# A decoder layer's opening: c sent to all partitions by DMA, a full-width first rstd row, TensorE on zeros, and two chunks instead of three

## The chip, the cores and the metric

One core of one Trainium2 chip. The metric is the device time of one execution in microseconds. TensorE is called PE (PEld for its weight loads), VectorE DVE, ScalarE ACT, GpSimd POOL, and SyncE, which issues every DMA of this kernel, SP.

## The reference

A decoder layer for 256 tokens of width 2048 in float32: a SwiGLU, a token mixer, a second SwiGLU, each behind an RMSNorm whose shift, scale and gate come from a conditioning vector c. Only the first SwiGLU's opening is touched:

```python
cond = jax.nn.silu(c)
mod = cond @ ada_w[l] + ada_b[l]            # 9 x 2048 numbers
sh1, sc1, gt1, ... = jnp.split(mod, N_MOD, axis=-1)
y = x * rsqrt(mean(x * x) + EPS) * norm_g   # per token
h = y * (1 + sc1) + sh1
x = x + 0.5 * gt1 * ((silu(h @ wg) * (h @ wu)) @ wd)
```

Here h is 256 x 2048, wg and wu are 2048 x 5632, wd is 5632 x 2048.

## The kernel before, in words

Activations stand feature-major: x is 16 slices (k = 0 to 15) of 128 features by 256 tokens. A float32 product is made of two parts each: hs holds each slice of h as a high and a low half, and each weight tile (128x128) is split into whi and wlo.

*Weights.* They come in blocks of 8 tiles, 512 KB, in the order of use (`Stream.next`): SP issues the DMA into `wraw`, ACT casts it to `whi` (L94), DVE subtracts to get `wlo` (L97). Each of the three rotates over three tiles, and every fourth block has a tile of its own, so a block reuses the place of the one four before it.

*adaLN columns.* A column is 128 numbers of mod. `ada_col` sends 1 MB of ada_w (128 features x 2048) by DMA and multiplies and sums it against silu(c), held in `cs` on all partitions, in one DVE pass (L204). The first four have tiles of their own (`adaf`); the others rotate over two (`adat`). The order is scale and shift of slice 0, of slice 1, and so on: 32 columns for SwiGLU_1's h, then the gates. Columns are recorded beside the weights at a rate per block (`RATE`, 0.45 at first), or at once where a slice is about to be used (`ada_need`). When a slice's second column is done, `modulate_one` makes it: the gain g (L302), ht = x times gain times the rstd row (L289), hs on ACT and its low half on DVE.

*First row.* Until then: c goes to one partition, POOL broadcasts it, ACT applies Silu. ACT squares x, DVE sums the squares to two slices, `norm_rstd` contracts them against two columns of ones into rstd as a column per token, and turns it into a row on all partitions by two more matmuls (L275, L276, copied in L281).

*The first half of SwiGLU_1* (`gate_up_first`, 28 feature groups f of 128, g and u each) contracts in chunks of slices, so that PE can begin before all of h is there: for each chunk all 28 f, in groups of 8 with a PSUM bank (`pgu`) each. In the first group of a chunk the first LEAD slices are taken slice by slice over all 8 f, the rest f by f. Between chunks a bank is evacuated to `acc`: by ACT after the first chunk (L436), by a DVE add after a middle one (L438), by two DVE adds and the Silu after the last. Each weight tile takes three matmuls of 256 columns (L423 to L425), so a block is 24 matmuls and the half is 112 blocks, 2688 matmuls. Then comes the down projection (`pd`).

The order on each engine is written by a scheduler when the kernel is built; each engine then runs its list in order, and SP issues its DMAs in order, waiting where a tile isn't free.

Of the kernel before, what the change touches and what calls it, by code (L numbers as in the profile page):

```python
# [8 lines left out]
F32 = mybir.dt.float32  # L9
F32R = mybir.dt.float32r  # L10
BF16 = mybir.dt.bfloat16
I32 = mybir.dt.int32
AF = mybir.ActivationFunctionType
ALU = mybir.AluOpType
PSUM = bass.MemoryType.PSUM

P = 128
D = 2048
T = 256
KD = D // P  # L20
FF = 5632
NF = FF // P
PARTS = ((0, 28, NF), (0, NF // 2, NF))
CHUNKS = (0, 2, 6, 16)
LEAD = (2, 2, 6)
NH = 8
HD = 128
EPS = 1e-6
# [7 lines left out]
N_FIRST = 4  # L36
AHEAD = 4
X_AT = 1
TILE_US = 0.32
HIDX = 3  # L40
MORE = True
# [67 lines left out]
def layer_kernel(ctx: ExitStack, tc: tile.TileContext, xt, c, adaw, cols, cst, w, out, order, dbg=None):  # L109
    nc = tc.nc  # L110
    V, A, G, PE = nc.vector, nc.scalar, nc.gpsimd, nc.tensor
# [6 lines left out]
    tmp = ctx.enter_context(tc.tile_pool(name="tmp", bufs=2))  # L118
# [5 lines left out]
    def psb(name="psb"):  # L124
        return big.tile([P, 512], F32, name=name, tag="psb")
# [4 lines left out]
    def psf(name="psf"):  # L130
        return sm2.tile([P, 512], F32, name=name, tag="psf")
# [6 lines left out]
    W = Stream(nc, w, raw, hi, lo)  # L138
# [3 lines left out]
    x = keep.tile([P, KD, T], F32, name="x")  # L142
# [2 lines left out]
    cstt = keep.tile([P, N_CST], F32, name="cstt")  # L145
    early = ExitStack()
    ep = early.enter_context(tc.tile_pool(name="early", bufs=1))
    crow = ep.tile([1, D], F32, name="crow")
    warm = ep.tile([P, 1], F32, name="warm")
    V.memset(warm, 0.0)  # L150
    A.activation(warm, warm, AF.Silu)
    nc.sync.dma_start(crow, c)
    nc.sync.dma_start(colt, cols)
    first_ada = []
    x_parts = [slice(0, 4), slice(4, 8), slice(8, 12), slice(12, 14), slice(14, 16)]
    for i in range(N_FIRST):
        if i == X_AT:
            for sl in x_parts:
                nc.sync.dma_start(x[:, sl], xt[:, sl])
        t = ep.tile([P, D], F32, name=f"adaf{i}")  # L160
        nc.sync.dma_start(t, adaw[i])
        first_ada.append(t)

    def C(name, lo_=0, n=None):
        o, wd = CST[name]
# [2 lines left out]
    def L(name, lo_=0, n=None):  # L168
        o, wd = COL[name]
        return colt[:, o + lo_ : o + (wd if n is None else lo_ + n)]  # L170

    ident = L("ident")
    for q in range(4):
        sl = slice(q * 512, (q + 1) * 512)
        G.partition_broadcast(cs[:, sl], crow[:, sl])
        A.activation(cs[:, sl], cs[:, sl], AF.Silu)


# [5 lines left out]
    ada_done = {}  # L184

    def ada_col():

        i = ada_st["i"]
        if i >= len(ada_seq):
            return  # L190
        ada_st["i"] += 1
        m, j = ada_seq[i]
        q = m * KD + j
        if first_ada:
            t = first_ada.pop(0)
        else:
            t = adap.tile([P, D], F32, name="adat")
            if W.last is None:
                nc.sync.dma_start(t, adaw[i])
            else:  # L200
                with tc.issue_after(W.last):
                    nc.sync.dma_start(t, adaw[i])
        with W.behind(False):
            V.tensor_tensor_reduce(t, t, cs, 1.0, L("adab", q, 1), ALU.mult, ALU.add, mod[:, q : q + 1])  # L204
        if (m, j) in ada_done:
            ada_done[m, j]()
# [30 lines left out]
    def sqrt_table(after):  # L237

        d = tiny.tile([P, 1], F32, name="dummy")
        return A.activation(d, after, AF.Sqrt, scale=0.0)  # L240
# [14 lines left out]
    def norm_rstd(keep_row=False):  # L255

        ps = psf("nsum")
        src = sqa["src"]
        for i, s in enumerate(src):
            for t in range(2):  # L260
                PE.matmul(ps[:, t * 2 : t * 2 + 2], s[:, t * P : (t + 1) * P], L("ones", 0, 2),
                          start=(i == 0 and t == 0), stop=(i == len(src) - 1), skip_group_check=True)
        y = tiny.tile([P, 2], F32, name="nstd")
        hv = tiny.tile([P, 2], F32, name="nhv")
        ya = tiny.tile([P, 2], F32, name="nya")
        A.activation(y, ps[:, 0:4:2], AF.Sqrt, bias=L("eps"), scale=1.0 / D)
        V.tensor_scalar(hv, ps[:, 0:4:2], -0.5 / D, -0.5 * EPS, ALU.mult, ALU.add)
        V.reciprocal(y, y)
        V.tensor_tensor(ya, y, y, ALU.mult)
        V.tensor_tensor(ya, ya, hv, ALU.mult)  # L270
        V.scalar_tensor_tensor(y, ya, 1.5, y, ALU.add, ALU.mult)
        rb = tmp.tile([P, 2, P], F32, name="rb", bufs=1)
        pr = psf("nrow")
        for t in range(2):
            last = V.tensor_scalar(rb[:, t], L("ones"), y[:, t : t + 1], None, ALU.mult)  # L275
            PE.matmul(pr[:, t * P : (t + 1) * P], rb[:, t], ident, start=True, stop=True)  # L276
        W.held = ([None, sqa["hold"]] if sqa["hold"] is not None else []) + [last.ins]
        if not keep_row:
            return pr[:, :T]
        row = tmp.tile([P, T], F32, name="nrow", bufs=1)  # L280
        V.tensor_copy(row, pr[:, :T])  # L281
        return row
# [123 lines left out]
    def gate_up_first(fs, hp):  # L406

        r = first_row
        for j in range(KD):
            ada_done[0, j] = lambda j=j: modulate_one(j, gains(0, 1, j, 1), mod[:, j : j + 1], r)  # L410
        W.hold, W.held = ada_done[0, 0]().ins, []
        for _ in range(2, N_FIRST):
            ada_col()
        groups = [fs[i : i + 8] for i in range(0, len(fs), 8)]
        chunks = list(zip(CHUNKS[:-1], CHUNKS[1:]))
        acc, hids = {}, []

        def three(ps, f, s, k, k0, k1):
            o = ps[:, s * T : (s + 1) * T]
            wh, wl = W.next(("gu"[s], 0), k, f)  # L420
            first, last = k == k0, k == k1 - 1
            skip = s == 1
            PE.matmul(o, wh, hs[:, k, 0], start=first and s == 0, stop=False, skip_group_check=skip)  # L423
            PE.matmul(o, wh, hs[:, k, 1], start=False, stop=False, skip_group_check=skip)  # L424
            PE.matmul(o, wl, hs[:, k, 0], start=False, stop=last, skip_group_check=skip)  # L425

        turn = [0]

        def bank():
            turn[0] += 1  # L430
            return psn(turn[0], "pgu")

        def evacuate(ps, f, ci):
            if ci == 0:
                acc[f] = hp.tile([P, 2 * T], F32, name="acc", tag="hid")
                A.copy(acc[f], ps)  # L436
            elif ci < len(chunks) - 1:
                V.tensor_add(acc[f], ps, acc[f])  # L438
            else:
                tg, tu = pt("tg"), pt("tu")  # L440
                V.tensor_add(tg, ps[:, :T], acc[f][:, :T])
                V.tensor_add(tu, ps[:, T:], acc[f][:, T:])
                hids.append(swi(tg, tu, hp))

        for ci, (k0, k1) in enumerate(chunks):
            for gi, grp in enumerate(groups):
                if gi == 0 and LEAD[ci]:
                    pb = {f: bank() for f in grp}
                    ks = k0 + LEAD[ci]
                    for k in range(k0, ks):  # L450
                        ada_need(0, k)
                        for f in grp:
                            for s in range(2):
                                three(pb[f], f, s, k, k0, k1)
                    for f in grp:
                        for k in range(ks, k1):
                            ada_need(0, k)
                            for s in range(2):
                                three(pb[f], f, s, k, k0, k1)
                        evacuate(pb[f], f, ci)  # L460
                else:
                    for f in grp:
                        pf = bank()
                        for k in range(k0, k1):
                            ada_need(0, k)
                            for s in range(2):
                                three(pf, f, s, k, k0, k1)
                        evacuate(pf, f, ci)
        return hids
# [27 lines left out]


    xsq = ep.tile([P, KD, T], F32, name="xsq")
    for _ in range(2):  # L500
        ada_col()
    tc.keep_in_program_order(sqrt_table(cs[:, :1]))
    for q, sl in enumerate(x_parts):
        n = sl.stop - sl.start
        if q == 3:
            V.tensor_add(xsq[:, :n], xsq[:, :n], xsq[:, n : 2 * n])
        A.activation(xsq[:, sl], x[:, sl], AF.Square)
        if q:
            W.hold = V.tensor_add(xsq[:, :n], xsq[:, :n], xsq[:, sl]).ins
    sqa["src"] = [xsq[:, k] for k in range(2)]  # L510
    first_row = norm_rstd(keep_row=True)
    early.close()
    if dbg is None or "ffn1" in dbg:
        ffn(0, 0, 1, 2)
# [596 lines left out]
```

## Time and profile before

| | us |
|---|---|
| median of 3 runs (lowest, highest) | 2140.96 (2139.41, 2142.0) |
| the profiled execution | 2140.64 |
| its span, first to last instruction | 2138.8 |
| first pgu matmul | 27.24 |
| first pd matmul | 370.93 |

Mean granted TensorE clock 0.988. Rows of a timeline give start, duration, engine, line, operation, output <- inputs, count, and in brackets the idle time before and what ended it. Rows by stage give the busy time and the count of instructions of each engine in it. A matmul's own duration contains its filling and draining; the distance of two starts is its cost in a stream.

### The profile page before, as it was taken

Reading aid. Unit: us, or ns where it says so; the run is one execution under the profiler, and the core shown is the slowest. Engines: PE = TensorE matmul, PEld = TensorE weight load, DVE = VectorE, ACT = ScalarE, POOL = GpSimd, SP = SyncE. Lnnn points to the kernel's source line nnn. Section 1 sums busy time; section 2 is a strip of 40 time slices with the busy share of each in tenths; the row PEclk is TensorE's granted clock in tenths of the full one; section 3 lists DMA queues with packets and bytes.
Section 4 is the critical chain, followed back from the end, with each engine's and each line's share of the span. In section 5 each row is a group of like instructions: output and inputs, shape, how many; then the busy total and the mean of one; then the engine's idle time right before and its main releaser. Section 6 shows DMA issues by size and latency. Waiting matters only on the chain.

```text
span 2138.8 us, 32869 instructions
## 1 busy us (share of the span) xinstructions
PE 2048.0 (96%) x12530; PEld 1812.6 (85%) x12530; DVE 1612.2 (75%) x2516; ACT 1035.0 (48%) x1674; POOL 141.7 (7%) x161
## 2 busy tenths in 40 slices
PE   5999999999999999999999999999999999999997
PEld 4998999888888878777877887788888888888886
DVE  6899877888888977788888887776666555555555
ACT  5534444333444447555655654454444334444442
POOL 0000000000000010211221101100000000000011
PEclk9999999999999999999999999999999999999998
DMA  8989767999998875555555567666665555555553
GB/s 310 334 337 342 285 237 273 329 342 342 328 335 336 327 257 175 204 186 182 183 180 183 190 223 276 226 236 239 233 240 195 187 187 189 193 190 187 190 188 114
DMA packets 123584, 518.26 MB, mean 242 GB/s; under 512 B 13722, under 2 KB 15770, under 8 KB 104994
## 3 DMA queue, kind: packets, MB, share of 16 engines
q1 hardware_dynamic: 123426, 516.17, 67.6%
q8 instruction: 98, 1.61, 0.3%
q14 instruction: 60, 0.48, 0.1%
HBM read 511.91 MB, written 4.21 MB: 241 GB/s over the span
## 4 chain that ended last, share of the span: by engine, by line
PE 81%; DVE 10%; DMA 4%; issue 2%; ACT 2%; POOL 0%; DVEq 0%; ACTq 0%; SPq 0%
PE pd L353 15%; PE pg L353 10%; PE pu L353 10%; PE pd L354 8%; PE pp L353 6%; PE pu L354 5%; PE pg L354 5%; PE pp L354 3%; PE pgu L425 3%; PE pgu L423 3%; PE pgu L424 3%; DVE wlo L97 3%; DVE adat L204 2%; PE po L353 2%; DMA adat<-in_ada_dram 2%
## 5 line engine op out<-in xcount | busy, mean ns | idle before, releaser
L97 DVE TENSOR_TENSOR wlo<-wraw,whi 128x1024 fp32r<-128x1024 f32 x674 | 825.0, 1228 | 344.5 <-ACT whi L94 343.3
L94 ACT CAST whi<-wraw 128x1024 fp32r<-128x1024 f32 x674 | 705.9, 1049 | 770.7 <-issue 207.0
L353 PE MATMUL pd<-hid,whi 128*128 128x512 f32 x1408 | 492.2, 393 | 0.0
L354 PE MATMUL pd<-hid,wlo 128*128 128x256 f32 x1408 | 393.2, 279 | 0.2 <-DVE wlo L97 0.2
L204 DVE CUSTOM_DVE_ANT_0 adat<-adat,cs,colt 128x2048 f32<-128x2048 f32 x140 | 336.4, 2403 | 52.5 <-DMA adat<-in_ada_dram 52.1
L353 PE MATMUL pg<-hs,whi 128*128 128x512 f32 x960 | 339.9, 394 | 2.2 <-DVE hs L296 1.8
L353 PE MATMUL pu<-hs,whi 128*128 128x512 f32 x960 | 340.2, 395 | 0.0
L353 PEld LDWEIGHTS pd<-hid,whi 128*128 128x128 f32 x1408 | 263.7, 187 | 61.9 <-DVE hid L368 0.3
L353 PE MATMUL pp<-hs,whi 128*128 128x512 f32 x784 | 293.2, 408 | 1.8 <-DVE hs L296 1.8
L354 PE MATMUL pu<-hs,wlo 128*128 128x256 f32 x960 | 269.5, 281 | 0.0
L354 PE MATMUL pg<-hs,wlo 128*128 128x256 f32 x960 | 269.4, 281 | 0.0
L354 PEld LDWEIGHTS pd<-hid,wlo 128*128 128x128 f32 x1408 | 264.4, 188 | 0.5 <-DVE wlo L97 0.5
L423 PE MATMUL pgu<-hs,whi 128*128 128x256 f32 x896 | 255.2, 286 | 7.3 <-ACT whi L94 7.0
L425 PE MATMUL pgu<-hs,wlo 128*128 128x256 f32 x896 | 251.8, 286 | 8.0 <-DVE wlo L97 7.9
L424 PE MATMUL pgu<-hs,whi 128*128 128x256 f32 x896 | 254.5, 285 | 0.0
L354 PE MATMUL pp<-hs,wlo 128*128 128x256 f32 x784 | 232.6, 297 | 0.0
L353 PEld LDWEIGHTS pg<-hs,whi 128*128 128x128 f32 x960 | 180.6, 188 | 43.7 <-issue 2.1
L353 PEld LDWEIGHTS pu<-hs,whi 128*128 128x128 f32 x960 | 180.5, 188 | 41.5
L354 PEld LDWEIGHTS pg<-hs,wlo 128*128 128x128 f32 x960 | 181.9, 189 | 0.5 <-DVE wlo L97 0.4
L354 PEld LDWEIGHTS pu<-hs,wlo 128*128 128x128 f32 x960 | 181.9, 189 | 0.1
L423 PEld LDWEIGHTS pgu<-hs,whi 128*128 128x128 f32 x896 | 173.6, 194 | 8.7 <-ACT whi L94 7.9
L425 PEld LDWEIGHTS pgu<-hs,wlo 128*128 128x128 f32 x896 | 171.1, 193 | 10.5 <-DVE wlo L97 10.3
(268 smaller groups left out, 2256.8 us busy)
## 6 DMA issues: line engine op xcount, KB each, us to landing
wraw<-in_w_dram SPq DMA_DIRECT2D x674, 512.0 KB, 4.1
adat<-in_ada_dram SPq DMA_DIRECT2D x140, 1024.0 KB, 7.1
adaf<-in_ada_dram SPq DMA_DIRECT2D x4, 1024.0 KB, 12.5
xd<-x SPq DMA_DIRECT2D x4, 512.0 KB, 6.5
rw<-rows SPq DMA_DIRECT2D x16, 128.0 KB, 6.1
x<-xd SPq DMA_DIRECT2D x4, 512.0 KB, 6.1
out_dram<-o SPq DMA_DIRECT2D x8, 256.0 KB, 2.2
x<-in_x_dram SPq DMA_DIRECT2D x3, 512.0 KB, 7.3
```

Of the source, the lines that this page charges most:

```text
L94: nc.scalar.copy(self.h, r)
L97: nc.vector.tensor_tensor(self.l, r, self.h.bitcast(F32), ALU.subtract)
L204: V.tensor_tensor_reduce(t, t, cs, 1.0, L("adab", q, 1), ALU.mult, ALU.add, mod[:, q : q + 1])
L353: PE.matmul(ps, wt[0], act.rearrange("p a t -> p (a t)"), start=first, stop=False)
L354: PE.matmul(ps[:, :T], wt[1], act[:, 0], start=False, stop=last)
L423: PE.matmul(o, wh, hs[:, k, 0], start=first and s == 0, stop=False, skip_group_check=skip)
L424: PE.matmul(o, wh, hs[:, k, 1], start=False, stop=False, skip_group_check=skip)
L425: PE.matmul(o, wl, hs[:, k, 0], start=False, stop=last, skip_group_check=skip)
```

## The change

The vector c is read by one DMA onto all 128 partitions, straight into cs; POOL's broadcast is gone, and Silu takes two passes. The second column's transfer stands behind x, those of the third and fourth behind the first weights. The squares go to two sums of four slices; eight matmuls against a full square of ones give the sum of squares on all partitions, and sqrt, reciprocal and a Newton step work on 128x256. PE multiplies zeros (26 and 8 matmuls of 512 columns) ahead of that. The chunks 0-2, 2-6, 6-16 become 0-3, 3-16, with a LEAD of 3 and 9. The wait that put the first wlo behind the first slice is now at the next block, and the second pair of columns is no longer made ahead of the first weights.

```diff
-CHUNKS = (0, 2, 6, 16)
-LEAD = (2, 2, 6)
+CHUNKS = (0, 3, 16)
+LEAD = (3, 9)
...
+N_WARM = (26, 8)
...
-    crow = ep.tile([1, D], F32, name="crow")
...
-    nc.sync.dma_start(crow, c)
-    nc.sync.dma_start(colt, cols)
+    zw = ep.tile([P, 512], BF16, name="zw")
+    V.memset(zw, 0.0)
+    zp = psb("zp")
+    def warm_up(n):
+        for _ in range(n):
+            PE.matmul(zp, zw[:, :P], zw, start=True, stop=True)
+    warm_up(N_WARM[0])
+    nc.sync.dma_start(cs, c.broadcast_to([P, D]))
...
-    x_parts = [slice(0, 4), slice(4, 8), slice(8, 12), slice(12, 14), slice(14, 16)]
+    x_parts = [slice(4 * i, 4 * i + 4) for i in range(4)]
     for i in range(N_FIRST):
         if i == X_AT:
+            nc.sync.dma_start(colt, cols)
             for sl in x_parts:
                 nc.sync.dma_start(x[:, sl], xt[:, sl])
         t = ep.tile([P, D], F32, name=f"adaf{i}")
-        nc.sync.dma_start(t, adaw[i])
         first_ada.append(t)
+        if i < 2:
+            nc.sync.dma_start(t, adaw[i])
...
-    for q in range(4):
-        sl = slice(q * 512, (q + 1) * 512)
-        G.partition_broadcast(cs[:, sl], crow[:, sl])
+    for q in range(2):
+        sl = slice(q * 1024, (q + 1) * 1024)
         A.activation(cs[:, sl], cs[:, sl], AF.Silu)
...
             t = first_ada.pop(0)
+            if i >= 2:
+                nc.sync.dma_start(t, adaw[i])
...
-        W.hold, W.held = ada_done[0, 0]().ins, []
-        for _ in range(2, N_FIRST):
-            ada_col()
+        W.hold, W.held = None, [ada_done[0, 0]().ins]
...
-    for _ in range(2):
-        ada_col()
-    tc.keep_in_program_order(sqrt_table(cs[:, :1]))
+    ada_col()
     for q, sl in enumerate(x_parts):
-        n = sl.stop - sl.start
-        if q == 3:
-            V.tensor_add(xsq[:, :n], xsq[:, :n], xsq[:, n : 2 * n])
         A.activation(xsq[:, sl], x[:, sl], AF.Square)
-        if q:
-            W.hold = V.tensor_add(xsq[:, :n], xsq[:, :n], xsq[:, sl]).ins
-    sqa["src"] = [xsq[:, k] for k in range(2)]
-    first_row = norm_rstd(keep_row=True)
+        if q % 2:
+            V.tensor_add(xsq[:, sl], xsq[:, sl], xsq[:, 4 * q - 4 : 4 * q])
+    tc.keep_in_program_order(sqrt_table(x[:, KD - 1, :1]))
+    ps = psf("nsum")
+    for q in (1, 3):
+        for k in range(4 * q, 4 * q + 4):
+            PE.matmul(ps[:, :T], L("ones"), xsq[:, k], start=(k == 4), stop=(k == KD - 1))
+    warm_up(N_WARM[1])
+    first_row = ep.tile([P, T], F32, name="frow")
+    fy = ep.tile([P, T], F32, name="fy")
+    fh = ep.tile([P, T], F32, name="fh")
+    A.activation(fy, ps[:, :T], AF.Sqrt, bias=L("eps"), scale=1.0 / D)
+    V.tensor_scalar(fh, ps[:, :T], -0.5 / D, -0.5 * EPS, ALU.mult, ALU.add)
+    V.reciprocal(fy, fy)
+    V.tensor_tensor(first_row, fy, fy, ALU.mult)
+    V.tensor_tensor(first_row, first_row, fh, ALU.mult)
+    row = tmp.tile([P, T], F32, name="nrow", bufs=1)
+    V.scalar_tensor_tensor(row, first_row, 1.5, fy, ALU.add, ALU.mult)
+    first_row = row
+    ada_col()
```

DVE's list around the first slice, before (ISA rows of 128x2048 are column passes; the row of 128x1 behind each reads its sum):

```order
L204 ISA adaf_105,mod<-adaf_105,cs,colt 128x2048
L204 ISA mod 128x1
L267 TENSOR_SCALAR nhv<-nsum 128x2
L268 RECIPROCAL nstd<-nstd 128x2
L269 TENSOR_TENSOR nya<-nstd 128x2
L270 TENSOR_TENSOR nya<-nya,nhv 128x2
L271 SCALAR_TENSOR_TENSOR nstd<-nya,nstd 128x2
L275 TENSOR_SCALAR rb<-colt,nstd 128x128 x2
L281 COPY nrow<-nrow 128x256
L289 SCALAR_TENSOR_TENSOR ht<-x,g_165,nrow 128x256
L296 SCALAR_TENSOR_TENSOR hs<-ht,mod,hs 128x256
L204 ISA adaf_107,mod<-adaf_107,cs,colt 128x2048
```

The same place now:

```order
L216 ISA adaf_132,mod<-adaf_132,cs,colt 128x2048
L216 ISA mod 128x1
L525 TENSOR_SCALAR fh<-nsum 128x256
L526 RECIPROCAL fy<-fy 128x256
L527 TENSOR_TENSOR frow<-fy 128x256
L528 TENSOR_TENSOR frow<-frow,fh 128x256
L530 SCALAR_TENSOR_TENSOR nrow<-frow,fy 128x256
L301 SCALAR_TENSOR_TENSOR ht<-x,g_185,nrow 128x256
L308 SCALAR_TENSOR_TENSOR hs<-ht,mod,hs 128x256
L98 TENSOR_TENSOR wlo<-wraw,whi 128x1024 x2
L216 ISA adaf_134,mod<-adaf_134,cs,colt 128x2048
```

The row is made at 256 columns without the second pass through PE, and two wlo now stand ahead of the third column. The second place is DVE's list at the weight blocks 34 to 36, before:

```order
L97 TENSOR_TENSOR wlo<-wraw,whi 128x1024
L438 TENSOR_TENSOR acc<-pgu,acc 128x512
L97 TENSOR_TENSOR wlo<-wraw,whi 128x1024
L204 ISA adat,mod<-adat,cs,colt 128x2048
L204 ISA mod 128x1
L438 TENSOR_TENSOR acc<-pgu,acc 128x512
L302 SCALAR_TENSOR_TENSOR g_1456<-mod,colt 128x1
L97 TENSOR_TENSOR wlo<-wraw,whi 128x1024
L289 SCALAR_TENSOR_TENSOR ht<-x,g_1456,nrow 128x256
L438 TENSOR_TENSOR acc<-pgu,acc 128x512
```

And now:

```order
L98 TENSOR_TENSOR wlo<-wraw,whi 128x1024
L216 ISA adat,mod<-adat,cs,colt 128x2048
L216 ISA mod 128x1
L98 TENSOR_TENSOR wlo<-wraw,whi 128x1024
L308 SCALAR_TENSOR_TENSOR hs<-ht,mod,hs 128x256
L216 ISA adat,mod<-adat,cs,colt 128x2048
L216 ISA mod 128x1
L314 SCALAR_TENSOR_TENSOR g_1522<-mod,colt 128x1
L301 SCALAR_TENSOR_TENSOR ht<-x,g_1522,nrow 128x256
L98 TENSOR_TENSOR wlo<-wraw,whi 128x1024
```

The adds into acc are gone, and a column follows each wlo, where before one column stood in these three blocks.

## The prediction

> **What bounds the kernel now.** I read the page first: one core, TensorE (PE) busy almost throughout.
>
> ```profile
> span 2138.8 us, 32869 instructions
> PE 2048.0 (96%) x12530; PEld 1812.6 (85%) x12530; DVE 1612.2 (75%) x2516; ACT 1035.0 (48%) x1674; POOL 141.7 (7%) x161
> ```
>
> So a change of the opening can only pay through PE's idle or slow time there. Second, the first half of SwiGLU_1 alone (tile pgu, 2688 matmuls) by stage; columns: stage, its length, then busy us and count of PE, PEld, DVE, (ACT), granted clock, DMA share, GB/s.
>
> ```profile
> 27.00:35.00 8.00, 5.78 (x25) 5.49 (x26) 0.00 (x0) 0.00 (x0) 1.00 0.18 62
> 35.00:60.00 25.00, 25.00 (x209) 25.00 (x208) 0.00 (x0) 10.26 (x18) 1.00 0.90 345
> 180.00:190.00 10.00, 10.00 (x86) 10.00 (x86) 0.00 (x0) 0.00 (x0) 1.00 0.88 331
> 190.00:200.00 10.00, 8.32 (x52) 7.63 (x50) 0.00 (x0) 0.00 (x0) 0.83 0.91 340
> 200.00:205.00 5.00, 2.25 (x10) 1.83 (x9) 0.00 (x0) 0.00 (x0) 0.78 0.94 334
> 260.00:300.00 40.00, 40.00 (x337) 40.00 (x336) 3.75 (x10) 0.00 (x0) 1.00 0.73 261
> ```
>
> The count, not the busy time, tells the speed: 337 in 40 us is 0.12 us a matmul; 25 in 8 us and 62 in the 15 us from 190 to 205 are the two holes. Third, the matmuls themselves, at the start and at the end of this half:
>
> ```profile
> 27.24 0.58 PE L423 MATMUL pgu<-hs,whi 128*128 128x256 f32 x1 [2.51 <-ACT whi L94]
> 27.83 0.41 PE L423 MATMUL pgu<-hs,whi 128*128 128x256 f32 x1
> 28.04 0.41 PE L424 MATMUL pgu<-hs,whi 128*128 128x256 f32 x1
> ...
> 370.70 0.28 PE L424 MATMUL pgu<-hs,whi 128*128 128x256 f32 x1
> 370.82 0.28 PE L425 MATMUL pgu<-hs,wlo 128*128 128x256 f32 x1
> 370.93 0.40 PE L353 MATMUL pd<-hid,whi 128*128 128x512 f32 x1
> ```
>
> The half starts at 27.24, with matmuls 0.21 us apart, and the down projection starts at 370.93. At 0.12 us, 2688 matmuls take 322.6 us, so 21.1 us are lost inside. Fourth, VectorE (DVE) in the second hole:
>
> ```profile
> 184.26 2.35 DVE L204 CUSTOM_DVE_ANT_0 adat<-adat,cs,colt 128x2048 f32<-128x2048 f32 x1
> 186.53 0.09 DVE L204 DVE_READ_ACCUMULATOR2_ANT mod<- 128x1 f32 x1
> 186.58 1.23 DVE L97 TENSOR_TENSOR wlo<-wraw,whi 128x1024 fp32r<-128x1024 f32 x1
> 187.72 0.42 DVE L293 TENSOR_TENSOR hs<-ht,hs 128x256 fp32r<-128x256 f32 x1
> 188.47 2.35 DVE L204 CUSTOM_DVE_ANT_0 adat<-adat,cs,colt 128x2048 f32<-128x2048 f32 x1 [0.34 <-DMA adat<-in_ada_dram]
> 190.75 0.08 DVE L204 DVE_READ_ACCUMULATOR2_ANT mod<- 128x1 f32 x1
> 190.87 0.16 DVE L302 SCALAR_TENSOR_TENSOR g<-mod,colt 128x1 f32<-128x1 f32 x1
> 191.06 0.48 DVE L289 SCALAR_TENSOR_TENSOR ht<-x,g,nrow 128x256 f32<-128x256 f32 x1
> 192.14 2.35 DVE L204 CUSTOM_DVE_ANT_0 adat<-adat,cs,colt 128x2048 f32<-128x2048 f32 x1 [0.60 <-DMA adat<-in_ada_dram]
> ...
> 203.86 0.42 DVE L293 TENSOR_TENSOR hs<-ht,hs 128x256 fp32r<-128x256 f32 x1
> 204.65 2.35 DVE L204 CUSTOM_DVE_ANT_0 adat<-adat,cs,colt 128x2048 f32<-128x2048 f32 x1 [0.37 <-DMA adat<-in_ada_dram]
> ```
>
> Here PE waits for the last slice of h: hs 15 is done at 204.3. Each slice needs two adaLN columns, and DVE makes them at a pitch of (204.65-184.26)/5 = 4.08 us. From start to start a column costs 2.35 us, a wlo 1.14, g and ht about 0.6, the hs rest 0.37; between those two columns stand 5 columns, 3 wlo, 2 pairs, 3 hs, 17.5 us of work in 20.4, a factor of 1.17, since only two adat tiles rotate. Their transfers in this stretch, and all of DVE from the first matmul to hs 15:
>
> ```profile
> DMA to landing us min/median/max: 5.5/6.5/8.3
> ...
> L97 DVE TENSOR_TENSOR wlo<-wraw,whi 128x1024 fp32r<-128x1024 f32 x57 | 68.8, 1221 | 7.5 <-ACT whi L94 7.2
> L438 DVE TENSOR_TENSOR acc<-pgu,acc 128x512 f32<-128x512 f32 x28 | 19.1, 688 | 1.3 <-PE pgu L425 0.8
> ```
>
> **The change, part by part.** A block is one weight load of 8 tiles, 24 matmuls, 2.88 us. The prologue, before:
>
> ```profile
> 8.28 2.80 POOL L175 PARTITION_BROADCAST cs<-crow  x4 [7.83 <-issue]
> 13.15 3.97 ACT L507 ACTIVATE xsq<-x 128x1024 f32<-128x1024 f32 x5
> 20.10 1.87 PE L261 MATMUL nsum<-colt,xsq 128*128 128x2 f32 x8 [20.10 <-DVE xsq L509]
> 23.50 1.23 PE L276 MATMUL nrow<-colt,rb 128*128 128x128 f32 x4 [1.53 <-DVE rb L275]
> 24.76 0.42 DVE L281 COPY nrow<-nrow 128x256 f32<-128x256 f32 x1 [1.12 <-PE nrow L276]
> 25.74 0.51 ACT L295 ACTIVATE hs<-ht,mod 128x256 fp32r<-128x256 f32 x1 [3.47 <-DVE ht L289]
> ```
>
> The weight cast on ScalarE (ACT), from the page, and the DMA supply at that time (columns as in the stages above, with POOL):
>
> ```profile
> L94 ACT CAST whi<-wraw 128x1024 fp32r<-128x1024 f32 x674 | 705.9, 1049 | 770.7 <-issue 207.0
> 10.00:15.00 5.00, 0.00 (x0) 0.00 (x0) 2.52 (x3) 4.91 (x7) 1.07 (x2) 1.00 1.02 413
> ```
>
> *c by DMA.* GpSimd's late broadcast (8.28 to 11.1) goes; 1.05 MB of extra transfer comes. The queue moves 0.413 MB a us from about 2 us on. Ahead of the end of x now stand cs 1.05, one column 1.05, colt 0.31, x 2.10 MB: landed at 2+10.9+about 1 = 14; the second column at 16.5, the first weights at 18. So Silu is early and the queue is the limit.
>
> *First row at full width.* The last square ends at 15, its DVE add (1.2, as a wlo of the same size) at 16.3. Eight ones-matmuls of 256 columns: four records of 128 columns took 1.23 us, so the last four cost 1.7 to 3.4; I take 3: 19.3. The second column holds DVE from 16.5 to 18.9. In ACT's queue a weight cast stands ahead of the Sqrt; 18 plus 1.05 is covered. Sqrt 0.5 (an ACT pass of 256 columns, as hs), then reciprocal, two products, the row and ht, about 0.4 each (nrow's copy, 0.42) is 2.0, hs 0.5: with 1.2 of hand-overs the first pgu matmul is at 23.5. The wide reciprocal's only row is two elements in 0.16; between 0.4 and a wlo's 1.2 I take 0.4, the copy being of its size. The start lies between 21.5 and 26.5: 3.7 us earlier, 0.7 to 5.7.
>
> *PE on zeros.* All 34 stand in PE's order ahead of the ones-matmuls: even at the 0.43 us that 512 columns take at the opening's spacing (2 x 0.21) they end before 16.3, so they delay nothing. *Whether the clock is still up.* Here 25 matmuls ran at 0.21 instead of 0.12: 2.3 us, the most a warm start is worth. But slice k=1 then comes 9.9 us after slice 0, while 48 matmuls need 5.8 us fast and 10.2 slow: the gain stays at 0 to 0.3, hidden. In the Trainium skill, "TensorE: Matmul & The Clock Gate", section "What's actually happening", the clock falls back after an idle window of about 3.4 us; by it the zeros, done long before 23.5, leave PE cold and the sum has 0 here, warm it would have at most that 2.3. The slow spacing at 27.24, after PE's idle stretch, agrees.
>
> *Chunks 0-3, 3-16.* Removed: 28 adds into acc, 0.6 us from start to start on DVE (19.1 us busy), and no work on PE. Moved: k=3 and later are wanted 7 blocks later, k=6 to 15 some 15 blocks earlier. In the opening DVE does, between hs 0 and hs 1, three wlo, two columns, g, ht: 8.8 us, plus ACT 1.1, against 5.8 on PE: 4.1 us idle; for k=2 2.8 likewise; 2 more for transfers that wait for the two adat tiles. 23.5 + 21 x 2.88 + 8.9 = 92.9 is when PE reaches block 21. Weight tiles go round in fours, so DVE cannot be past wlo 24 then: 94. From there its order holds, up to hs 15: 17 columns, 18 wlo, 8 pairs, 9 hs = 40.0+20.5+4.8+3.3 = 68.6 us. If no transfer were waited for: 162.6. By the factor 1.17: 80.3, hs 15 at 174.3. If each column took (8.3+2.35)/2 = 5.3 us: 90, 184. I take 174.3, since that stretch has the same mix and the same two tiles.
>
> By PE's order 56 of the 96 matmuls of blocks 39 to 42 can run before it needs hs 15: 73 x 24 - 56 = 1696 are left, 203.5 us. Before, 58 x 24 - 38 = 1354 were left at 204.3, 162.5 us, and 370.93 came 4.1 us later than that; the same 4.1 is kept. The new end is 174.3 + 203.5 + 4.1 = 381.9, 11.0 us later. **Sum:** the profiled execution, 2140.64 us (span 2138.8 and 1.8 around it; the median of the runs is 2140.96), becomes 2151.6; I say 2152. What follows is unchanged and only shifts; some six columns are made earlier there, off PE's path. Break-even is hs 15 at 163.3, because leaving 342 more matmuls behind it costs 41 us.
>
> **Rivals.** *A, transfers hidden (no change).* The two tiles suffice, DVE alone bounds: hs 15 at 162.6 to 166, 2140 to 2143.5. For it: DVE was short of adat by under 1 us each time; against: the 1.17. In the Trainium skill, "DMA: Bandwidth & Descriptors", section "Anatomy of one DMA — SWDGE (gpsimd) path", a DMA costs about 2 us plus bytes at 436 GB/s; that is 4.4 us here, an estimate, a pitch of 3.4 us, and this rival would hold. The 5.5 to 8.3 us above, on another queue, speak against it.
> *B, faster.* The start decides: first matmul at 20.5, k=1 and k=2 without idle, block 21 at 87, hs 15 at 157 by DVE's work alone: 2134 to 2136. It needs both, a prologue 3 us better than my sum and no adat wait; decided at hs 15 before 159. Against it: three of the four terms of the opening's idle are DVE's own work.
> *C, slower still.* The broadcast read or the wide row is slow, the start at 26.5, pitch 5.3: hs 15 at 187, 2164.
>
> **The numbers.** Forecast 0.64 (2146 to 2160), C 0.10, A 0.13, B 0.13. 0.2% is 4.3 us, about what a measurement of this kernel tells from no change: faster 0.13, same 0.13, slower 0.74. The range, 2137 to 2165, leaves out most of B and the far end of C. The likeliest alone: 2146 to 2160.
>
> **What would show it.** First pgu matmul at 21.5 to 26.5; PE 4 us idle before k=1; PE at full pace from about 45 to 110; then a hole of 20 to 30 us, columns at about 4.1 us, hs 15 near 174; pd starting near 382; no acc adds on DVE. I am wrong if hs 15 is done by 163, or if the pitch falls to DVE's own 3.9 or less.

## The result, and the profile after

| | before | after |
|---|---|---|
| median of 4 runs each (lowest, highest), us | 2140.18 (2133.89, 2142.0) | 2159.68 (2156.14, 2162.57) |
| ratio to before, 95% interval | | 1.0096 (1.0069 to 1.0122) |
| profiled execution, span, us | 2140.64, 2138.8 | 2158.37, 2156.3 |
| mean granted clock | 0.988 | 0.980 |

The kernel became 1% slower; 2152 was forecast, with 2137 to 2165 as the range. The head of the page after:

```profile
span 2156.3 us, 32917 instructions
PE 2066.0 (96%) x12568; PEld 1822.8 (85%) x12568; DVE 1599.9 (74%) x2483; ACT 1036.9 (48%) x1671; POOL 139.0 (6%) x157
```

PE's share is the 96% of before, and its busy time rose by 18 us: 9.5 of them are the zeros and 2.5 the wider ones-matmuls. Another 8.4 lie in the first half of SwiGLU_1, with the same 2688 matmuls: its granted clock is 0.95 instead of 0.99, and a pgu matmul at half clock is recorded with 0.41 us instead of 0.28. Behind that half PE is busy 2.4 us less. So the busy share hides the loss; the counts by stage show it. Tile pgu in the kernel after, with the columns of the prediction's stage rows:

```profile
27.00:35.00 8.00, 6.05 (x42) 5.85 (x42) 0.00 (x0) 0.00 (x0) 0.86 0.68 278
60.00:100.00 40.00, 39.63 (x332) 39.42 (x331) 0.00 (x0) 9.40 (x16) 1.00 0.91 343
150.00:200.00 50.00, 32.04 (x166) 29.40 (x167) 4.51 (x12) 0.00 (x0) 0.69 0.87 326
260.00:300.00 40.00, 40.00 (x338) 40.00 (x337) 3.76 (x10) 0.00 (x0) 1.00 0.67 227
```

The same 50 us of the kernel before:

```profile
150.00:200.00 50.00, 48.32 (x387) 47.63 (x385) 2.06 (x3) 0.00 (x0) 0.97 0.93 347
```

The opening is ahead (42 matmuls against 25 from 27 to 35 us), but by 45 us that lead is gone (108 matmuls done, 107 before); the middle runs at full pace, and from 150 to 200 there are 166 matmuls in place of 387. At 0.12 us a matmul that hole is 30 us wide, with a granted clock of 0.69. Three rows of the timeline of the kernel after give its edges: the second row ends when hs 15 is done, at 176.67.

```profile
159.02 0.58 PE L433 MATMUL pgu<-hs,whi 128*128 128x256 f32 x1 [5.59 <-ACT whi L95]
...
176.25 0.42 DVE L305 TENSOR_TENSOR hs<-ht,hs 128x256 fp32r<-128x256 f32 x1
...
389.90 0.40 PE L365 MATMUL pd<-hid,whi 128*128 128x512 f32 x1
```

The down projection starts 19.0 us later than before (370.93). From there to the end of the span it is 1766.4 us, against 1767.9: the whole loss lies in the first half of SwiGLU_1. A stage from hs 15 to the first pd matmul counts what was left behind that slice; after, and then before:

```profile
176.67:389.90 213.23, 207.76 (x1696) 206.64 (x1695) 20.32 (x54) 0.00 (x0) 0.98 0.77 284
```

```profile
204.28:370.93 166.65, 163.42 (x1353) 162.37 (x1352) 20.24 (x54) 0.00 (x0) 0.99 0.74 268
```

After: 1696 x 0.12 = 203.5 of 213.2 us, 9.7 lost. Before: 162.4 of 166.65, 4.3 lost. So hs 15 came 27.6 us earlier, 41 us more of work stood behind it, and 5.4 us more went astray there: +19.

### The profile page after: what moved, and what is told of

It reads as the page before. It is cut to its first block, busy times and chain, and to the rows that moved or that the text cites. A ratio compares the mean times of both kernels' runs of the same rounds, so it can differ in the third digit from the quotient of the medians.

```text
span 2156.3 us, 32917 instructions
## 1 busy us (share of the span) xinstructions
PE 2066.0 (96%) x12568; PEld 1822.8 (85%) x12568; DVE 1599.9 (74%) x2483; ACT 1036.9 (48%) x1671; POOL 139.0 (6%) x157
## 4 chain that ended last, share of the span: by engine, by line
PE 83%; DVE 9%; DMA 4%; issue 2%; ACT 2%; POOL 0%; SPq 0%; DVEq 0%; ACTq 0%
PE pd L365 15%; PE pg L365 10%; PE pu L365 10%; PE pd L366 8%; PE pp L365 6%; PE pu L366 5%; PE pg L366 5%; PE pgu L435 4%; PE pgu L434 4%; PE pgu L433 4%; PE pp L366 3%; DMA adat<-in_ada_dram 2%; DVE adat L216 2%; PE po L365 2%; DVE wlo L98 2%
```

## Experiments

Each ratio is to the kernel before on the same chip; the medians of before in the three batches were 2136.72, 2136.32 and 2137.32. "Lost behind hs 15" is the time from hs 15 to the first pd matmul, less 0.12 us for each matmul counted in it. These columns are of one profile each. From pd to the end of the span the profiles take 1767.9 us before and 1766.4 after, but 1759.1 (before, new chunks) to 1775.2 (third adat tile) in the others, with the same matmuls; so a few us at pd need not show in the ratio. Why that stretch varies is open.

| kernel | first pgu | hs 15 done | pd starts | matmuls left | lost behind hs 15 | ratio (95%) |
|---|---|---|---|---|---|---|
| before | 27.24 | 204.3 | 370.9 | 1353 | 4.3 | 1 |
| after | 24.93 | 176.7 | 389.9 | 1696 | 9.7 | 1.0096 (1.0069 to 1.0122) |
| after, once more | 24.11 | 178.3 | 393.9 | 1696 | 12.0 | 1.0108 (1.0092 to 1.0123) |
| after, old chunks | 24.85 | 204.7 | 370.2 | 1354 | 3.0 | 1.0012 (0.9999 to 1.0026) |
| before, new chunks | 26.92 | 181.4 | 396.6 | 1696 | 11.7 | 1.0115 (1.0101 to 1.0130) |
| after, third adat tile | 23.99 | 166.8 | 383.9 | 1732 | 9.2 | 1.0108 (1.0092 to 1.0125) |
| after, no zeros | 25.52 | 178.2 | 390.4 | 1695 | 8.8 | 1.0115 (1.0101 to 1.0129) |
| after, fewer gate columns | 24.36 | 178.6 | 388.8 | 1696 | 6.6 | 1.0084 (1.0070 to 1.0098) |
| after, LEAD 11 | 24.02 | 176.9 | 383.9 | 1640 | 10.2 | 1.0076 (1.0061 to 1.0091) |
| after, 0-3, 3-8, 8-16 | 26.18 | 221.5 | 359.8 | 1150 | 0.4 | 0.9947 (0.9932 to 0.9962) |
| same, columns at 0.4 | 24.69 | 230.1 | 359.7 | 1036 | 5.3 | 0.9938 (0.9925 to 0.9950) |
| same (0.45), no zeros | 25.37 | 223.0 | 361.3 | 1150 | 0.3 | 0.9947 (0.9933 to 0.9961) |
| before, 0-3, 3-8, 8-16 | 27.83 | 224.6 | 363.0 | 1150 | 0.3 | 0.9959 (0.9947 to 0.9972) |

### The change in its two parts

The new prologue with the old chunks:

```diff
-CHUNKS = (0, 3, 16)
-LEAD = (3, 9)
+CHUNKS = (0, 2, 6, 16)
+LEAD = (2, 2, 6)
```

> The changed kernel with the chunks of before (0-2, 2-6, 6-16): the new prologue alone. Theory 1 (the early need for columns is the whole loss): first pgu matmul near 24.9 us instead of 27.2, the hole before slice 15 as before, the down projection at 368 to 370, time 2 us below before, 0.998 to 1.000 of it. Rival (the prologue, with the zeros and the wide row, costs something itself): at or above before, 1.002 or more.

And the kernel before with the new chunks:

```diff
-CHUNKS = (0, 2, 6, 16)
-LEAD = (2, 2, 6)
+CHUNKS = (0, 3, 16)
+LEAD = (3, 9)
```

> The kernel before with the chunks 0-3, 3-16 alone. Theory 1: hs 15 near 178, the down projection at 390 to 393, 19 to 22 us above before (ratio 1.009 to 1.010). Rival (the prologue costs): near before, within 5 us.

Rows of the new prologue with the old chunks, PE's timeline:

```profile
24.85 0.80 PE L433 MATMUL pgu<-hs,whi 128*128 128x256 f32 x2 [5.12 <-ACT hs L307]
...
370.19 0.40 PE L365 MATMUL pd<-hid,whi 128*128 128x512 f32 x1
```

PE began 2.4 us earlier than before, and pd 0.7 us: with the old chunks the prologue is worth nothing that can be measured (1.0012, 0.9999 to 1.0026). That lies between the two expectations. The kernel before with the new chunks, from its hs 15 on:

```profile
181.39:396.57 215.18, 208.96 (x1696) 207.69 (x1695) 20.28 (x54) 0.00 (x0) 0.97 0.76 280
```

It is as slow as the whole change (1.0115), so the loss is the chunks' alone. Hs 15 came 3.4 us later than I expected, and pd 3.6 later than the end of its range; pd is 25.6 us later than before, while its profiled span is 16.9 longer.

### A third tile for the columns

Is the 1.17 over DVE's own work the turnaround of two adat tiles? In SwiGLU_1 every third column gets a tile of its own; two hid tiles of SwiGLU_1 and a second buffer of a small tile make room.

```diff
-            t = adap.tile([P, D], F32, name="adat")
+            t = (third[0] if third and i % 3 == 0 else adap).tile([P, D], F32, name="adat")
...
-        g1 = tiny.tile([P, n], F32, name="g1", tag=f"g1{n}")
+        g1 = tiny.tile([P, n], F32, name="g1", tag=f"g1{n}", bufs=1 if n == KD else 2)
...
-        with tc.tile_pool(name=f"hid{which}", bufs=PARTS[which][1] + HIDX) as hp, \
+        with tc.tile_pool(name=f"hid{which}", bufs=PARTS[which][1] + (1 if which == 0 else HIDX)) as hp, \
```

> The changed kernel with a third rotating tile for the column transfers during SwiGLU_1 (paid for with two fewer hid tiles). Theory 1a (in the hole DVE waits for transfers because two tiles turn around too slowly): DVE's waits for adat there, 8 us, go, the column pitch falls from 4.2 to about 3.7 us, hs 15 comes at 165 to 169 instead of 176.7, time 7 to 11 us lower (ratio to before 1.004 to 1.006). Rival 1b (DVE's own work is the bound): unchanged within 2 us. Rival 1c (the DMA queue is full in the hole, at 345 GB/s): unchanged, with the waits moved to the weights.

Waits of the kernel after from 92 to 180 us (us in total, times, longest), then its DMA issues from 94 to 180:

```profile
DVE adat L216 <- DMA adat<-in_ada_dram: 8.2, 10, 1.4
ACT whi L95 <- DMA wraw<-in_w_dram: 50.4, 16, 7.1
PE pgu L433 <- ACT whi L95: 10.6, 4, 5.6
```

```profile
adat<-in_ada_dram SPq DMA_DIRECT2D x19, 1024.0 KB, 6.4
```

The hole before hs 15 is not only a wait for slices. SP issues in order, so a weight's transfer stands behind columns that wait for a free tile (from 145.8 to 159.3 us it issues four columns and one weight block): ACT's casts waited 50.4 us for their transfers, and PE's longest waits, 10.6 us in four, are for such casts. With the third tile these two are down to 27.3 and 1.7, and PE waits for hs instead, 10.7 us for ACT's part of it. DVE then waited for no column, and hs 15 and the rest came so:

```profile
166.41 0.42 DVE L306 TENSOR_TENSOR hs<-ht,hs 128x256 fp32r<-128x256 f32 x1
...
383.88 0.39 PE L366 MATMUL pd<-hid,whi 128*128 128x512 f32 x1
```

The 8.2 us of short waits are gone, and hs 15 is done at 166.8, 9.8 us earlier. Count from where the forecast's 68.6 us of DVE's work begin, behind the wlo of block 24, its 25th: that wlo was done at 99.6 here, and DVE needed 67.3 us to hs 15. Its own work was 67.5, the 68.6 less one wlo that now came after hs 15. So DVE now sets the pace itself. Pd started 6.0 us earlier. The total did not follow: from pd to the end of the span it took 2159.1 - 383.9 = 1775.2 us, 8.8 more than after. The tiles taken from hid may be a part of that; I didn't run it apart. They can't be all of it: from 1400 to 1600 us behind pd, in the second SwiGLU with its hid tiles as before, PE is busy throughout at a clock of 1.00 in both kernels, yet has 1134 matmuls in place of 1154, some 3.5 us. The cause is open. In the half itself the turnaround is shown; the kernel as a whole gained nothing.

### No zeros

```diff
-N_WARM = (26, 8)
+N_WARM = (0, 0)
```

> The changed kernel without the matmuls on zeros. Theory 1: PE's clock had fallen back to half before the first pgu matmul anyway, so at most the ones-matmuls slow down; within 2 us of the changed kernel (ratio to before 1.007 to 1.010). Rival (the zeros keep PE warm and are worth something): 2 to 4 us slower than the changed kernel. Rival (the zeros delay the row): faster by 1 us or more.

1.0115 (1.0101 to 1.0129) without the zeros, 1.0108 (1.0092 to 1.0123) with them in the repeated run: no difference. The rows of PE after show where the zeros end and how the first slice then ran:

```profile
1.22 9.51 PE L159 MATMUL zp<-zw 128*128 128x512 bf16 x34 [1.22 <-DVE zw L154]
14.21 5.60 PE L519 MATMUL nsum<-xsq,colt 128*128 128x256 f32 x16 [3.48 <-DVE xsq L514]
24.93 0.80 PE L433 MATMUL pgu<-hs,whi 128*128 128x256 f32 x2 [5.12 <-ACT hs L307]
...
34.84 1.21 PE L433 MATMUL pgu<-hs,whi 128*128 128x256 f32 x8 [1.95 <-ACT hs L304]
```

They end at 10.7, 14 us ahead of the first slice, and PE stands idle for 5.1 us right before it. And k=1 came 9.9 us after slice 0, with PE idle for the last 2 us, so a warm start would have been waited away. In the program 8 of the 34 stand behind the ones-matmuls, but the scheduler put all 34 ahead of them; zeros that last up to the first slice were not run.

### What the loss behind hs 15 is made of

The 9.7 us were more than twice the 4.1 of the forecast. Two stages of 23 us behind hs 15, all engines (PE, PEld, DVE, ACT, POOL), after and then before:

```profile
177.00:200.00 23.00, 17.99 (x109) 17.11 (x108) 21.59 (x35) 10.99 (x19) 0.00 (x0) 0.80 0.87 342
```

```profile
204.00:227.00 23.00, 20.44 (x156) 19.62 (x155) 22.12 (x40) 14.28 (x23) 0.00 (x0) 0.95 0.75 284
```

After, 109 matmuls are worth 13.1 us of pace: 9.9 of the 23 us are lost, so the whole loss is here. About 5.0 are idle; the other 4.9 are matmuls longer than 0.12, at a granted clock of 0.80. Rows of the two timelines show how an idle piece arises, DVE first, then ACT, then PE:

```profile
191.33 2.34 DVE L216 CUSTOM_DVE_ANT_0 adat<-adat,cs,colt 128x2048 f32<-128x2048 f32 x1
...
193.59 0.42 DVE L396 TENSOR_TENSOR tu<-tu,tg 128x256 f32<-128x256 f32 x1
```

```profile
194.05 0.40 ACT L379 CAST hid<-tu 128x256 fp32r<-128x256 f32 x1 [2.79 <-DVE tu L396]
...
194.77 1.03 ACT L95 CAST whi<-wraw 128x1024 fp32r<-128x1024 f32 x1
```

```profile
195.85 0.39 PE L433 MATMUL pgu<-hs,whi 128*128 128x256 f32 x1 [2.47 <-ACT whi L95]
```

Behind hs 15 the banks of the last chunk are evacuated, by adds on DVE and passes on ACT that wait for each other. A gate column (2.34 us) stands ahead of the product L396; ACT waits 2.79 us for that product, and the weight cast behind it in ACT's order is the one that PE waits for. Before, hs 15 came with (2688 - 1353) / 24 = 55.6 blocks begun, and from block 56 on columns are recorded at 0.2 a block; now it comes with 41.3 begun, and they go at 0.45 up to block 56. So the next run thins them there:

```diff
-RATE = ((0, 0.45), (56, 0.2), ...)
+RATE = ((0, 0.45), (40, 0.1), (56, 0.2), ...)
```

> The changed kernel with the columns recorded at 0.1 instead of 0.45 per weight block between blocks 40 and 56; the columns up to slice 15 are untouched, only those of the gates behind them move back. Open is the tail: from hs 15 to the first pd matmul the changed kernel loses 9.9 us over 0.12 us a matmul, the kernel before 4.5. If the gate columns there (on DVE and in the DMA queue) make that loss, it falls to about 5 and pd starts near 385, 5 us earlier (ratio to before 1.007). If it is the granted clock, which is 0.70 to 0.94 in that stretch, or the catching up of weights behind the hole, the tail stays 9 to 10, pd starts at 389 to 391 and the ratio at 1.009 to 1.011.

Columns (tile adat) in such a stage of 23 us behind hs 15: after, then this run.

```profile
177.00:200.00 23.00, 9.17 (x4) 0.80 0.87 342
```

```profile
179.00:202.00 23.00, 1.87 (x1) 0.87 0.75 280
```

With one column in place of four the loss fell to 6.6:

```profile
178.61:388.75 210.14, 206.16 (x1696) 205.09 (x1694) 20.24 (x54) 0.00 (x0) 0.99 0.69 250
```

The waits changed as the rows above suggest. In the stage after, ACT waited 8.7 us for DVE's tg and tu, PE 3.2 us for ACT's casts, and ACT only 0.2 us for a weight's transfer, so the queue is not the cause there; with one column the first two are 1.4 and 0.2. The loss is neither theory's number, but between them: the changed kernel itself gave 9.7 and 12.0 in two executions, and the other kernels with two chunks and the old rate 8.8 to 11.7. Pd started only 1.1 us earlier than after, since hs 15 came 1.9 later. The ratio, 1.0084 (1.0070 to 1.0098), overlaps with that of the repeated run, and most of what the profiled span gained on that of after, 7.0 us, lies behind pd. So the columns are a part of the loss, by one profile with fewer of them; how much precisely is open.

### The last slice wanted later

```diff
-LEAD = (3, 9)
+LEAD = (3, 11)
```

> The changed kernel with LEAD (3, 11) in place of (3, 9): in the first group of the second chunk 11 slices instead of 9 are taken slice by slice, so hs 15 is first wanted in block 43 instead of 39, and slices 12 and 13 two blocks later or earlier by little. My theory: the end of the half is hs 15 plus the matmuls left behind it; DVE makes hs 15 at the same 176 to 178, about 1600 matmuls (192 us) are left instead of 1694, so pd starts at 379 to 383, 8 to 10 us earlier than 389.9, and the time is about 2150, ratio to before 1.005. Rival: it is the total of DVE's and the queue's work, not where hs 15 is wanted, that sets the end; then pd stays at 388 to 391 and the ratio at 1.010.

```profile
176.90:383.92 207.02, 201.07 (x1640) 200.01 (x1639) 20.15 (x54) 0.00 (x0) 0.98 0.74 274
```

Hs 15 came at the same time, 176.9; 56 matmuls fewer were left behind it, 6.7 us, and pd started 6.0 us earlier than after, 9.9 earlier than in its repeat. The rival (no change) is out; I had expected some 94 matmuls fewer, and missed by that. The ratio, 1.0076 (1.0061 to 1.0091), is lower, but its interval overlaps with that of the first run of the change and ends just below that of the second.

### Three chunks with a later last one

```diff
-CHUNKS = (0, 3, 16)
-LEAD = (3, 9)
+CHUNKS = (0, 3, 8, 16)
+LEAD = (3, 3, 6)
```

> The changed kernel's prologue with three chunks, 0-3, 3-8, 8-16, LEAD (3, 3, 6): slices 8 to 15 are wanted from block 56 on, hs 15 not before block 68, where PE comes at about 24.9 + 9 + 68 x 2.88 = 230; the 28 adds into acc (19 us of DVE) are back. My theory: hs 15 is done by about 200 or a little later, the hole is gone, and the half lasts 322.6 us and 10 to 14 of losses: pd starts at 358 to 363, 8 to 13 us earlier than before, 2128 to 2133 in all, ratio 0.994 to 0.997. Rival: PE's idle time is only moved, by the adds on DVE and the bank changes, and what the half gains is given back behind it, as with the third adat tile: pd at 368 to 372 or the total at 2138 to 2142, ratio 0.999 to 1.001.

Tile pgu in this run, by stage, and then its half from hs 15 on:

```profile
100.00:150.00 50.00, 48.64 (x400) 47.71 (x399) 9.34 (x14) 0.00 (x0) 1.00 0.85 330
150.00:200.00 50.00, 49.83 (x412) 49.08 (x411) 9.59 (x14) 0.00 (x0) 1.00 0.82 315
```

```profile
221.49:359.84 138.35, 137.55 (x1150) 137.11 (x1148) 20.23 (x54) 0.00 (x0) 1.00 0.73 263
```

The hole is gone: 412 matmuls from 150 to 200, clock 1.00. Pd starts at 359.8, and the time is 2124.27 us, 0.9947 (0.9932 to 0.9962) of before. DVE does its 28 acc adds again and it costs PE little (812 matmuls from 100 to 200, 97.4 us at pace), because slice 15, done at 221.5, is no longer what PE waits for. This beats both kernels. The same with fewer columns in the opening:

```diff
-RATE = ((0, 0.45), (56, 0.2), ...)
+RATE = ((0, 0.4), (56, 0.2), ...)
```

> The run before with columns recorded at 0.4 instead of 0.45 per weight block up to block 56, so that fewer columns stand between the weights while PE is fed just in time. If the columns between the first weights cost PE time that slice 15 has to spare, pd starts 1 to 3 us earlier than with 0.45 and the time is 1 to 3 us lower. If slice 15 is already late at 0.45, it is 2 to 5 us slower. If neither is on PE's path, both agree within 0.1%.

2122.94 us, 0.9938 (0.9925 to 0.9950): not to be told from 0.45, pd at 359.7. In the two profiles this is a sum of two differences: PE lost 3.6 us less between its first pgu matmul and hs 15, and 4.9 more behind it, most of that in one wait for a wlo:

```profile
249.65 0.39 PE L435 MATMUL pgu<-hs,wlo 128*128 128x256 f32 x1 [4.31 <-DVE wlo L98]
```

Does that gain need the new prologue? The kernel before with these chunks alone (CHUNKS and LEAD as above):

> The kernel before, with nothing changed but CHUNKS (0, 3, 8, 16) and LEAD (3, 3, 6). Is the gain of these chunks theirs alone, or does it need the new prologue? With two chunks the new prologue brought pd forward by 6.7 us (396.6 to 389.9), because there slice 15 is what PE waits for. My theory: with three chunks slice 15 has some 10 us to spare, so a prologue that starts pgu 1 to 2 us later costs no more than that: pd at 360 to 363, the time 2123 to 2127, ratio to before 0.994 to 0.996. Rival: the prologue keeps its 5 to 7 us: pd at 365 to 367, ratio 0.997 to 0.998.

It ran at 0.9959 (0.9947 to 0.9972), pd at 363.0: 0.41% of the 0.53% are there without the new prologue. The prologue's share, 3.1 us at pd in one profile each, lies within the intervals. And without zeros (N_WARM = (0, 0)) on the run with the new prologue:

> The run with chunks 0-3, 3-8, 8-16 and the new prologue, without PE's multiplications of zeros. The first pgu matmuls came 0.21 us apart in most profiles with zeros, and without them the changed kernel was no slower. My theory: no effect, pd within 1.5 us of 359.8, ratio to before 0.993 to 0.996. Rival: where slice 15 no longer covers it, a warm start shows, up to 2.3 us: pd at 361 to 362, ratio 0.996 or more.

0.9947 (0.9933 to 0.9961), the ratio with them: the zeros are worth nothing here either.

### The change once more

> The changed kernel itself once more, to see how far its first half repeats: first pgu matmul 24.9, hs 15 at 176.7, pd at 389.9, 9.9 us lost behind hs 15, ratio to before 1.0096. If single profiles repeat, hs 15 and pd come within 2 us of these and the ratio at 1.008 to 1.011; if the 9.9 were an accident of that execution, the loss behind hs 15 falls to 4 to 7.

```profile
178.32:393.86 215.54, 209.00 (x1696) 207.74 (x1695) 20.32 (x54) 0.00 (x0) 0.97 0.76 280
```

1.0108 (1.0092 to 1.0123). Hs 15 repeated within 1.6 us, pd within 4.0, the difference being mostly the loss behind hs 15, 12.0. So the 9.7 were no accident, and a single profile tells that loss to some 2 us only.

## Why the prediction was right, and where it was off

*The direction and its cause: right.* It said that the chunks, not the prologue, decide, because slice 15 would come too late for the work moved behind it. The kernel before with new chunks shows the loss alone, LEAD 11 takes it back in part by changing only where that slice is wanted, and three chunks, which want it later still, take it back entirely.

*The size: little more than half.* The forecast was 11 us more, and the medians are 19.5 apart. Hs 15, pd and the time all came later than forecast; the range held because it left room for a worse start and pitch, and 2159.68 is just inside the likeliest 2146 to 2160. What was mis-sized is the loss behind hs 15 and, less, the start and hs 15 itself, which follow in the order of the path.

*The start, 23.5 against 24.93.* The mis-sized term is the wide reciprocal, taken at 0.4 us. On DVE:

```profile
20.69 1.74 DVE L526 RECIPROCAL fy<-fy 128x256 f32<-128x256 f32 x1
22.47 0.43 DVE L527 TENSOR_TENSOR frow<-fy 128x256 f32<-128x256 f32 x1
```

It took 1.74, four times the product behind it and beyond the 1.2 that I had as its upper end: 1.3 of the 1.4 us, the other terms' misses nearly cancelling. The start itself lay between 24.0 and 26.2 in the other profiles with this prologue, so a miss of 1.4 is within what single profiles differ by. In the Trainium skill, "VectorE: DVE Perf Modes", section "First, the fixed hardware budget", the reciprocal is said to be an iterative divide with a repeat count of 8; the row, four times a plain pass, fits that; the page has no price.

*The opening.* Slice k=1 came 9.9 us after slice 0, as summed; PE's 48 matmuls took part of that at 0.21 us, so it idled 2.0 us in place of 4.1. The first matmul of block 21 was forecast for 92.9; the count of PE's records gives 92.97.

*Hs 15, 174.3 against 176.7.* Two errors partly cancel here, which is luck. The sum lets DVE be past wlo 24 at 94, because PE then reaches block 21; PE did (92.97), but DVE was behind. It passed that wlo, the second of the two in the first row, at 99.0:

```profile
96.70 2.36 DVE L98 TENSOR_TENSOR wlo<-wraw,whi 128x1024 fp32r<-128x1024 f32 x2
98.97 2.35 DVE L216 CUSTOM_DVE_ANT_0 adat<-adat,cs,colt 128x2048 f32<-128x2048 f32 x1
```

From there DVE needed 77.7 us, 1.13 times the 68.6 in place of 1.17: 5.0 us later and 2.6 shorter. Of the 9.1 us over its own work 7.5 were waits for columns, and the third tile took them away, so the cause is the one named, the two tiles' turnaround, a little cheaper than taken. (The sign of columns every 4.1 us doesn't follow from the sum: 80.3 us for 17 columns is 4.7; it was 4.65.) The rival that transfers would be hidden is out. Its estimate from the Trainium skill, "DMA: Bandwidth & Descriptors", section "Anatomy of one DMA — SWDGE (gpsimd) path", was 4.4 us for 1 MB; in the stretch itself the median from issue to landing was 6.4, on SP's shared queue, so the trace does not agree.

*What was left, 1696 matmuls: exact.*

*The loss behind hs 15, kept at 4.1: the largest miss.* It was 9.7 and 12.0. I carried it over from before without looking at what stands behind hs 15 at its new place: gate columns at twice the rate among the evacuations, and PE coming out of a hole with the clock down (0.50 from 176 to 179 us). The run with fewer columns shows them to be a part of it; the clock's share was not run apart.

The sum: 2.4 + 5.6 = 8.0 us later at pd, less 1.2 behind it, is the step from 2151.6 to the 2158.4 of the profiled execution.

*The zeros: right.* They were costed at nothing, and are worth nothing in two pairs of kernels.

## What to carry to other kernels

Where a contraction is split so that it can begin before its last input is made, draw two lines: when the consumer reaches that input, and when the producer, at its real pitch and not its busy time, delivers it; the stage ends at the later of the two plus all work left behind it. Fewer chunks save evacuations on an engine with room and move all of that work behind the last slice; here the middle way, one slice late enough, was worth 0.5%, and an earlier start of PE next to nothing, since its second slice did not come earlier with it (hs 1 was done at 34.4 us before and 36.4 after). And a stall costs more than its idle time: look at what stands in the engines' queues right behind it, and at the clock.

## What was not expected of the hardware

The cost of short gaps in the clock. Rows of PE behind hs 15, kernel after:

```profile
182.75 0.28 PE L434 MATMUL pgu<-hs,whi 128*128 128x256 f32 x1
183.78 0.38 PE L433 MATMUL pgu<-hs,whi 128*128 128x256 f32 x1 [0.74 <-ACT whi L95]
184.00 0.28 PE L434 MATMUL pgu<-hs,whi 128*128 128x256 f32 x1
185.88 0.38 PE L435 MATMUL pgu<-hs,wlo 128*128 128x256 f32 x1 [1.61 <-DVE wlo L98]
...
186.44 0.42 PE L435 MATMUL pgu<-hs,wlo 128*128 128x256 f32 x1
186.66 0.41 PE L433 MATMUL pgu<-hs,whi 128*128 128x256 f32 x1
...
189.43 0.37 PE L434 MATMUL pgu<-hs,whi 128*128 128x256 f32 x1
189.64 0.28 PE L435 MATMUL pgu<-hs,wlo 128*128 128x256 f32 x1
189.75 0.28 PE L433 MATMUL pgu<-hs,whi 128*128 128x256 f32 x1
```

After two gaps of 0.74 and 1.61 us, with two matmuls between them, the granted clock fell from 1.00 (180 to 186 us) to 0.50 (187 to 189): from 186.2 to 189.4 the matmuls came 0.21 us apart, about 15 of them at 0.09 us extra, 1.4 us. In the Trainium skill, "TensorE: Matmul & The Clock Gate", section "What's actually happening", the clock falls back after an idle window of about 3.4 us and comes back after as long a busy one; the slow stretch of 3.2 us agrees, but the longest gap ahead of it was 1.61. The measurement decides: here 2.9 us (183.0 to 185.9) in which PE ran two matmuls went before the fall. With the slow stretch the 2.35 us of gaps cost 3.7.
